# A shorter inverse root in the norm, and weights, rows and empty steps placed otherwise, in a two-layer encoder

## The chip, the core and the metric

The kernel runs on one core of a Trainium2 chip. The metric is the device time of one execution in microseconds. A core has five engines that work side by side, each through its own queue of instructions in a fixed order: PE (TensorE, matrix products; its weight loads are shown as PEld), DVE (VectorE), ACT (ScalarE), POOL (GpSimd), and SP (SyncE), which here issues most of the transfers between memory and the core. An instruction starts when those ahead of it in its queue have been taken and what it waits for is there.

## The reference

Two groups of tokens, a prompt of 512 and a sample of 1024, pass through two layers with the same weights. All data are fp32 and 1024 features wide. One layer is:

```python
hn = rmsnorm(h, ln1[i])
z = hn @ w_in[i]
q, k, v, ga, uf, gf, mga, mgf = jnp.split(z, SPLIT_IDX, axis=-1)
a = band_attention(rope(q), rope(k), v, sink[i]) * jax.nn.silu(ga)   # 8 heads of 64, band of 128
f = fourier_mix(uf, w_fmix[i]) * jax.nn.silu(gf)                     # Re(FFT2) in 4 groups of 128
merged = sigmoid(mga) * (a @ w_ao[i]) + sigmoid(mgf) * (f @ w_fo[i])
h = h + merged @ w_out[i]
h = h + (p[i] @ w_pe[i]) * sigmoid(rmsnorm(h, ln_pg[i]) @ w_pg[i])
```

with `rmsnorm(x, g) = x * rsqrt(mean(x*x) + 1e-6) * g`, and a last rmsnorm behind the second layer.

## The kernel before

The tokens are three chunks of 512: chunk 0 is the prompt, chunks 1 and 2 are the sample and are called the pair. A tile is 128 features by 512 tokens, so a chunk has 8 tiles, and a weight of 128 outputs has 8 pieces of 128x128.

**Products in three parts.** An fp32 operand is split into a high part, cast by ACT (L89), and a low part, the difference from it, by DVE and for some weights by POOL (L90). A product is then three matmuls into one bank of PSUM: high by high (L101), high by low (L102), low by high (L103). So each weight and each activation needs one ACT and one DVE (or POOL) instruction of 128x512 before PE can use it. `Weights` does that for a stream of weights: `get` hands out weight i, loads weight i + 3 and splits weight i + 2 (L175 to L180).

**The stages.** In each layer come, in this order: the prompt's input projection with 34 weight tiles (`project_prompt`, some 45 to 285 us in layer 0 and 1142 to 1374 in layer 1); the pair's input projection (286 to 682, 1375 to 1771); and the merges of the branches, the output projection and the gate, first for the prompt, then for the pair, the pair's being the end of the program. The pair's projection multiplies its two chunks by two weight tiles at once in seven products instead of eight (L232), with the sums of weights S1 to S4 (L209 to L216) and the sums of activations T1 to T4 (`pair_parts`). `Pair.prepare(n)` makes and splits the weight operands up to the n-th of the order A11, S2, S1, S3, A12, A22, S4. `pair_made` makes the activations by rows: row k joins features k and k + 4 of the two chunks; it normalises four pieces (`pinned`, L390, or `normed`, L361) and makes seven operands. A product needs all four rows.

**Side work.** `run` lets a main generator go step by step and moves others along with it, each from a given step on and at a given rate. Beside the prompt's projection go, in turn, the pair's norm, rows 0 and 1, and then a chain of the prompt's attention, its Fourier part and row 2; row 3 comes behind the projection.

**The order on each engine.** The framework's scheduler puts the instructions of each engine in order by its own model of time; the order of the code is its priority. `keep_in_program_order` holds an instruction where the code has it (as in `pinned`), and `issue_after` lets it come only after a given one. Buffers are rings (45 tiles "act", 16 "scr", 12 "tiny", 20 "stat"), so an instruction can also wait for a buffer's last reader.

**The norm.** `Norm.add` sums the squares of the 8 tiles of a chunk. In `stats_steps` PE sums over features into a few columns (L333, L335), DVE computes the inverse root there, PE spreads it by transposes (L350), and DVE copies it (L356) for the normalisations. The inverse root is 12 operations on 128x4 or 128x2: adding eps (L339), a first guess from the bits (L341, L342), and three Newton steps of three operations (L344 to L346). There are 16 such chains in the program. The last chunk's tail is worked in two halves of 256 tokens, with its gate at L633 to L638 and its results at L662.

**Other names in the rows.** L371, L372, L378, L383: the sums of `pair_parts`. L420 to L423 (`roped`): the rotary embedding, of which L422 multiplies by the sines. L467, L468, L473: the gates of the prompt's projection. L828, L836, L863, L868: the attention's scores, their maximum, the transposes of the probabilities and the product with the values. L985 to L991: the Fourier part's products, L1046 its last sums on DVE and L1051 its gate on POOL. L239, L243, L249: sums of the pair's products. L598 to L602: gate and addition in the merges.

## Time and profile before

| what | value |
|---|---|
| runs | 2205.24, 2209.6, 2211.03 us; median 2209.6 |
| profiled execution | 2210.05 us, of which the span that the profile shows is 2208.3 |
| PE, matmuls | 2167.4 us busy, 98% of the span |
| DVE | 1501.5 us, 68% |
| ACT | 1090.1 us, 49% |
| POOL | 297.3 us, 13% |
| mean granted clock of PE | 0.995 of full speed |
| moved by transfers | 380.71 MB, mean 172 GB/s |

The profile is of one execution. A row of a timeline gives the start of a group of like instructions in us from the span's start, how long the group lasts, the engine, the line of the kernel, the operation, its output and inputs by pool (act, scr, tiny, misc, mm, sc, o), the shape, and the number of instructions; in brackets stands the engine's idle time just before and what ended it. Matmuls overlap in the pipeline, so a row lasts longer than the distance to the next. PE is the busiest engine by far, and the others matter where PE waits for them.

### The profile page before, as it was taken

What the parts mean: (1) busy time and instruction counts of PE and PEld (TensorE: products, weight loads), DVE (VectorE), ACT (ScalarE), POOL (GpSimd) and SP (SyncE); (2) the same over time, 40 slices, a digit from 0 to 9 for tenths busy, and PEclk for the clock granted to TensorE, in tenths of its full rate; (3) what the DMA queues carried; (4) which work ended last, traced back from release to release, by engine and by line L of the source; (5) the groups of instructions that cost most, each with busy time, mean ns of one, the idle gap of its engine ahead of it and who ended that gap; (6) DMA issues with size and microseconds to landing.
All of it is one profiled execution on the core that took longest, in us unless ns stands there. A gap on an engine that the chain in (4) does not pass through costs nothing. (4 is left out here: it accounts for less than half of the span.)

```text
span 2208.3 us, 30143 instructions
## 1 busy us (share of the span) xinstructions
PE 2167.4 (98%) x10242; PEld 1803.6 (82%) x10242; DVE 1501.5 (68%) x2896; ACT 1090.1 (49%) x2333; POOL 297.3 (13%) x216
## 2 busy tenths in 40 slices
PE   9999999999999999999999999999999999999997
PEld 7778877888888887888888888788888888888886
DVE  5866676776778883464557665867766787864386
ACT  5476433666665454124324854336666644612352
POOL 0201100000002111312400010100000011241141
PEclk9999999999999999999999999999999999999998
DMA  8565554444448575632356555443444574753143
GB/s 316 202 191 196 172 169 163 167 131 150 148 143 289 202 257 183 218 105 65 137 162 208 156 186 180 162 163 129 155 145 153 200 273 146 250 201 119 60 146 100
DMA packets 242170, 380.71 MB, mean 172 GB/s; under 512 B 21216, under 2 KB 97632, under 8 KB 242016
## 3 DMA queue, kind: packets, MB, share of 16 engines
q1 hardware_dynamic: 235104, 366.19, 49.1%
q10 hardware_dynamic: 6912, 12.59, 1.5%
q8 instruction: 81, 1.33, 0.2%
q14 instruction: 73, 0.60, 0.1%
HBM read 270.17 MB, written 108.53 MB: 171 GB/s over the span
## 5 line engine op out<-in xcount | busy, mean ns | idle before, releaser
L232 PE MATMUL mm<-act,act 128*128 128x512 f32 x2856 | 693.5, 393 | 7.1 <-ACT act L89 3.7
L232 PEld LDWEIGHTS mm<-act,act 128*128 128x128 f32 x2856 | 530.4, 188 | 117.2 <-ACT act L89 6.9
L101 PE MATMUL mm<-act,act 128*128 128x512 f32 (+1 forms) x1392 | 546.3, 393 | 6.2 <-ACT act L89 1.8
L103 PE MATMUL mm<-act,act 128*128 128x512 f32 (+1 forms) x1392 | 545.3, 392 | 3.7 <-DVE act L90 3.7
L102 PE MATMUL mm<-act,act 128*128 128x512 f32 (+1 forms) x1392 | 544.1, 391 | 0.0
L89 ACT CAST act<-act 128x512 fp32r<-128x512 f32 x574 | 329.5, 619 | 196.4 <-DMA act<-in_w_af 60.1
L90 DVE TENSOR_TENSOR act<-act,act 128x512 fp32r<-128x512 f32 x474 | 330.6, 732 | 24.3 <-ACT act L89 22.8
L103 PEld LDWEIGHTS mm<-act,act 128*128 128x128 f32 x1392 | 262.6, 189 | 60.1 <-DVE act L90 7.5
L101 PEld LDWEIGHTS mm<-act,act 128*128 128x128 f32 x1392 | 262.8, 189 | 59.6 <-ACT act L89 2.8
L102 PEld LDWEIGHTS mm<-act,act 128*128 128x128 f32 x1392 | 262.6, 189 | 51.5
L89 ACT CAST act<-scr 128x512 fp32r<-128x512 f32 (+1 forms) x260 | 152.9, 615 | 132.9 <-DVE scr L423 69.6
L90 DVE TENSOR_TENSOR act<-scr,act 128x512 fp32r<-128x512 f32 x256 | 179.1, 720 | 55.0 <-ACT act L89 53.7
L90 POOL TENSOR_TENSOR act<-act,act 128x512 fp32r<-128x512 f32 x100 | 142.8, 1453 | 324.4 <-ACT act L89 292.8
L321 ACT ACTIVATE scr<-act 128x512 f32<-128x512 f32 x103 | 63.8, 632 | 216.7 <-DVE act L582 142.9
L877 POOL TENSOR_TENSOR scr<-scr,scr 128x512 f32<-128x512 f32 x24 | 34.0, 1415 | 873.1 <-DVE scr L874 828.6
L90 DVE TENSOR_TENSOR act<-misc,act 128x512 fp32r<-128x512 f32 x132 | 88.2, 686 | 71.9 <-ACT act L89 71.7
L89 ACT CAST act<-misc 128x512 fp32r<-128x512 f32 x132 | 73.8, 587 | 122.2 <-PE misc L863 120.5
L839 ACT ACTIVATE act<-act,stat 128x385 f32<-128x385 f32 (+1 forms) x192 | 110.5, 579 | 35.8 <-DVE stat L836 35.2
L836 DVE CUSTOM_DVE_ANT_0 act<-sc,mask_sb,nsink_sb 128x384 f32<-128x384 f32 (+1 forms) x192 | 104.4, 569 | 32.1 <-PE sc L828 31.6
L101 PE MATMUL sc<-act,act 128*128 128x512 f32 (+1 forms) x316 | 118.6, 375 | 1.2 <-ACT scr L785 1.2
L102 PE MATMUL sc<-act,act 128*128 128x512 f32 (+1 forms) x316 | 118.1, 374 | 0.0
L103 PE MATMUL sc<-act,act 128*128 128x512 f32 (+1 forms) x316 | 117.9, 373 | 0.0
(222 smaller groups left out, 2622.2 us busy)
## 6 DMA issues: line engine op xcount, KB each, us to landing
act<-in_w_in SPq DMA_DIRECT2D x136, 256.0 KB, 4.7
act<-in_w_in SPq DMA_DIRECT2D x68, 512.0 KB, 4.4
gt<-scr SPq DMA_DIRECT2D x96, 256.0 KB, 2.7
scr<-gt SPq DMA_DIRECT2D x96, 256.0 KB, 5.4
act<-in_w_pg SPq DMA_DIRECT2D x80, 256.0 KB, 3.8
act<-in_w_af SPq DMA_DIRECT2D x64, 256.0 KB, 5.4
act<-in_w_out SPq DMA_DIRECT2D x64, 256.0 KB, 4.9
pl<-scr ACTq DMA_DIRECT2D x48, 256.0 KB, 3.0
```

The lines of the kernel that those rows point to most:

```text
L89: S.copy(hi, src)
L90: lo_eng.tensor_tensor(lo, src, f(hi), op=ALU.subtract)
L101: keep(PE.matmul(out, wh, xh, start=i == 0, stop=False))
L102: PE.matmul(out, wh, xl, start=False, stop=False)
L103: PE.matmul(out, wl, xh, start=False, stop=i == n - 1)
L232: PE.matmul(bank, w, v, start=first and k == 0 and n == 0, stop=k == 3 and n == 2, skip_group_check=True)
L321: S.activation(sq, h, AF.Square)
L836: V.tensor_tensor_reduce(out=pr[:, :W], in0=sc[:, :W], in1=msk, scale=-0.125, scalar=nsink_sb[:, l, head : head + 1], op0=ALU.add, op1=ALU ...
L839: S.activation(pr, pr, AF.Exp, bias=nmx[:, e], scale=-1.0, accum_out=rs[:, e])
L877: G.tensor_tensor(a2, a2, gate, op=ALU.mult)
```

## The change

- `Weights.get` splits weight i + 2 before it issues the load of weight i + 3; before, it was the other way round.
- `Norm`: eps is added once, in one of the wide accumulations on DVE (there is a flag for it), and the inverse root takes 8 small operations instead of 12: a first guess in one operation, one step of higher order with fitted constants in four, and one Newton step in three. It uses one more small tile.
- `pair_normed`: the normalisations of row 2 keep the place that the code gives them, as those of rows 0 and 1 do. Before, they were only held behind the row before.
- `roped`: the product with the sines (L422) of the pair's chunks goes to DVE; the prompt's stays on POOL. That is 8 instructions.
- In the prompt's attention four empty steps stand behind the first unit's scores.
- `first_weights` prepares the pair's first weight operands up to S3 in its last step, where before it stopped at S2.
- In `run`, rows 0 and 1 start at step 30 instead of 24, and the chain that begins with attention at step 42 instead of 44.

```diff
--- before.py
+++ after.py
@@ -175,8 +175,8 @@
         def get(self):
             i = self.at
             self.at += 1
+            self.split(i + 2)
             self.load(i + 3)
-            self.split(i + 2)
             return self.w.pop(i)
 
     class Pair:
@@ -310,7 +310,7 @@
 
     class Norm:
         def __init__(self):
-            self.acc = None
+            self.acc, self.has_eps = None, False
 
         def add(self, h, eng=V):
             if self.acc is None:
@@ -319,7 +319,11 @@
             else:
                 sq = scr()
                 S.activation(sq, h, AF.Square)
-                eng.tensor_tensor(self.acc, self.acc, sq, op=ALU.add)
+                if eng is V and not self.has_eps:
+                    V.scalar_tensor_tensor(self.acc, self.acc, D * EPS / P, sq, op0=ALU.add, op1=ALU.add)
+                    self.has_eps = True
+                else:
+                    eng.tensor_tensor(self.acc, self.acc, sq, op=ALU.add)
 
         def stats(self):
             for _ in self.stats_steps(range(4)):
@@ -334,16 +338,20 @@
                 if rest is not None:
                     PE.matmul(st[:, i : i + 1], rest[:, i * P : (i + 1) * P], mean_sb, start=False, stop=True)
 
-            v, y, z = (st[:, 4 * j : 4 * j + n] for j in range(1, 4))
-            self.r = r = sbt([P, n], F32, "tiny")
-            yield keep(V.tensor_scalar(v, st[:, 0:n], EPS, None, op0=ALU.add))
-
-            yield keep(V.tensor_scalar(y.bitcast(I32), v.bitcast(I32), 1, None, op0=ALU.arith_shift_right))
-            yield keep(V.tensor_scalar(r.bitcast(I32), y.bitcast(I32), -1.0, float(0x5F3759DF), op0=ALU.mult, op1=ALU.add))
-            for _ in range(3):
-                yield keep(V.tensor_tensor(z, v, r, op=ALU.mult))
-                yield keep(V.scalar_tensor_tensor(z, z, -0.5, r, op0=ALU.mult, op1=ALU.mult))
-                yield keep(V.scalar_tensor_tensor(r, z, 1.5, r, op0=ALU.add, op1=ALU.mult))
+            v, z, w = st[:, 0:n], st[:, 4 : 4 + n], st[:, 8 : 8 + n]
+            assert self.has_eps
+            self.r, q = sbt([P, n], F32, "tiny"), sbt([P, n], F32, "tiny")
+            r = self.r
+
+
+            yield keep(V.tensor_scalar(r.bitcast(I32), v.bitcast(I32), -0.5, float(0x5F113500), op0=ALU.mult, op1=ALU.add))
+            yield keep(V.tensor_tensor(z, v, r, op=ALU.mult))
+            yield keep(V.tensor_tensor(q, z, r, op=ALU.mult))
+            yield keep(V.scalar_tensor_tensor(w, q, -2.25339258, q, op0=ALU.add, op1=ALU.mult))
+            yield keep(V.scalar_tensor_tensor(r, w, 2.28257789, r, op0=ALU.add, op1=ALU.mult))
+            yield keep(V.tensor_tensor(z, v, r, op=ALU.mult))
+            yield keep(V.scalar_tensor_tensor(z, z, -0.5, r, op0=ALU.mult, op1=ALU.mult))
+            yield keep(V.scalar_tensor_tensor(r, z, 1.5, r, op0=ALU.add, op1=ALU.mult))
 
         def scale_ps(self, rb_ps, n=4):
             for j in range(n):
@@ -395,7 +403,7 @@
             hs = [[tile(i, kk) for i in range(2)] for kk in (k, k + 4)]
             for j in range(2):
                 for i in range(2):
-                    if k < 2:
+                    if k < 3:
                         pinned(hs[j][i], k + 4 * j, gain, rbs[i])
                     else:
                         with tc.issue_after(x["last"]):
@@ -419,7 +427,7 @@
             a, b = scr(), scr()
             V.tensor_tensor(a, out, self.rope[c, i][:, 0, :], op=ALU.mult)
             V.stream_shuffle(b, out, [j ^ 8 if i else j ^ 1 for j in range(32)])
-            G.tensor_tensor(b, b, self.rope[c, i][:, 1, :], op=ALU.mult)
+            (V if c else G).tensor_tensor(b, b, self.rope[c, i][:, 1, :], op=ALU.mult)
             V.tensor_tensor(a, a, b, op=ALU.add)
             return halves(a, V)
 
@@ -894,6 +902,9 @@
             yield from scores(u)
             if u:
                 yield from values(u - 1)
+            else:
+                for _ in range(4):
+                    yield
         yield
         yield from values(len(units) - 1)
 
@@ -1150,12 +1161,12 @@
             yield
             pairs.prepare(0)
             yield
-            pairs.prepare(1)
+            pairs.prepare(3)
 
         run(project_prompt(l, parts, ws, first_weights()), [
             (make, 8 if l == 0 else 10, 0.7 if l == 0 else 0.35),
-            (pair_made(xs, l, range(2)), 24, 1.0),
-            (chain(attention(l, (0,), False), fourier(l, 0), pair_made(xs, l, range(2, 3))), 4 * MT_U + 4, 2.1),
+            (pair_made(xs, l, range(2)), 30, 1.0),
+            (chain(attention(l, (0,), False), fourier(l, 0), pair_made(xs, l, range(2, 3))), 4 * MT_U + 2, 2.1),
         ])
         for _ in pair_made(xs, l, range(3, 4)):
             pass
```

Lines of the changed kernel from the norm on are higher by 8: L356 is L364, L390 is L398, L361 is L369, L371, L372, L378, L383 are L379, L380, L386, L391, and L468 is L476; L1046 is L1057.

The first place is DVE in the prompt's projection of layer 0, around 96 us. act_890 and act_885 are the raw tenth weight tile of w_in (before and now), and the two L90 that read it are its low parts; scr_870 and scr_877, now scr_861 and scr_868, are the pair's spread inverse roots. Before:

```order
L390 SCALAR_TENSOR_TENSOR act_623<-act_623,ln_sb,scr_877 128x512
L390 SCALAR_TENSOR_TENSOR act_631<-act_631,ln_sb,scr_877 128x512
L90 TENSOR_TENSOR act_918<-act_621,act_918 128x512
L371 TENSOR_TENSOR scr_916<-act_623,act_621 128x512
L372 TENSOR_TENSOR scr_917<-act_631,scr_916 128x512
L378 TENSOR_TENSOR act_623<-act_631,act_623 128x512
L468 SCALAR_TENSOR_TENSOR scr_935<-scr_935,mm_899 128x512
L468 SCALAR_TENSOR_TENSOR scr_988<-scr_988,mm_950 128x512
L468 SCALAR_TENSOR_TENSOR scr_1037<-scr_1037,mm_1004 128x512
L90 TENSOR_TENSOR act_938<-scr_917,act_938 128x512
L90 TENSOR_TENSOR act_944<-act_890,act_944 128x512
L90 TENSOR_TENSOR act_947<-act_890,act_947 128x512
```

Now:

```order
L90 TENSOR_TENSOR act_879<-act_802,act_879 128x512
L90 TENSOR_TENSOR act_882<-act_802,act_882 128x512
L90 TENSOR_TENSOR act_918<-act_885,act_918 128x512
L90 TENSOR_TENSOR act_921<-act_885,act_921 128x512
L364 COPY scr_861<-misc_856 128x512
L364 COPY scr_868<-misc_863 128x512
L398 SCALAR_TENSOR_TENSOR act_618<-act_618,ln_sb,scr_861 128x512
L476 SCALAR_TENSOR_TENSOR scr_915<-scr_915,mm_888 128x512
L398 SCALAR_TENSOR_TENSOR act_620<-act_620,ln_sb,scr_868 128x512
L398 SCALAR_TENSOR_TENSOR act_626<-act_626,ln_sb,scr_861 128x512
L398 SCALAR_TENSOR_TENSOR act_628<-act_628,ln_sb,scr_868 128x512
L476 SCALAR_TENSOR_TENSOR scr_959<-scr_959,mm_927 128x512
```

The two subtractions of the tenth tile stood behind the first row's pieces and three gates; now they stand behind those of the ninth tile (act_802) and ahead of the copies.

The second place is DVE at the end of the prompt's projection of layer 0, from 281 us on. scr_2904 and scr_2984 are S1 and S3 before, scr_2895 and scr_2905 are S1 and S3 now; scr_2944, scr_2943, act_627, act_633, act_635 belong to the pair's last row (now scr_2943, scr_2942, act_624 and so on). Before:

```order
L378 TENSOR_TENSOR act_627<-act_635,act_627 128x512
L213 TENSOR_TENSOR scr_2984<-act_2835,act_2836 128x512
L90 TENSOR_TENSOR act_2950<-scr_2944,act_2950 128x512
L90 TENSOR_TENSOR act_2953<-scr_2943,act_2953 128x512
L90 TENSOR_TENSOR act_2957<-act_627,act_2957 128x512
L90 TENSOR_TENSOR act_2960<-act_633,act_2960 128x512
L383 TENSOR_TENSOR act_633<-act_633,scr_2944 128x512
L243 TENSOR_TENSOR scr_3018<-mm_2979,scr_3001 128x512
L90 TENSOR_TENSOR act_2964<-act_633,act_2964 128x512
L90 TENSOR_TENSOR act_2967<-act_635,act_2967 128x512
L90 TENSOR_TENSOR act_2981<-scr_2904,act_2981 128x512
L90 TENSOR_TENSOR act_2986<-scr_2984,act_2986 128x512
```

Now:

```order
L210 TENSOR_TENSOR scr_2896<-scr_2895,act_2826 128x512
L213 TENSOR_TENSOR scr_2905<-act_2826,act_2827 128x512
L90 TENSOR_TENSOR act_2899<-scr_2896,act_2899 128x512
L90 TENSOR_TENSOR act_2902<-scr_2895,act_2902 128x512
L216 TENSOR_TENSOR scr_2896<-act_2826,scr_2896 128x512
L90 TENSOR_TENSOR act_2907<-scr_2905,act_2907 128x512
L90 TENSOR_TENSOR act_2944<-act_622,act_2944 128x512
L379 TENSOR_TENSOR scr_2942<-act_624,act_622 128x512
L380 TENSOR_TENSOR scr_2943<-act_632,scr_2942 128x512
L386 TENSOR_TENSOR act_624<-act_632,act_624 128x512
L90 TENSOR_TENSOR act_2949<-scr_2943,act_2949 128x512
L90 TENSOR_TENSOR act_2952<-scr_2942,act_2952 128x512
```

The low parts of S1 and S3 stood behind the whole last row; now they stand ahead of it, right behind that of S2 (scr_2896).

The third place is DVE at the end of the prompt's Fourier part, around 247 us: act_625, act_627, act_633, act_635 are the four pieces of row 2 before, and act_622, act_624, act_630, act_632 now. Before, their first normalisations stood in the work of row 1, at 115 us:

```order
L90 TENSOR_TENSOR act_1111<-act_629,act_1111 128x512
L383 TENSOR_TENSOR act_629<-act_629,scr_1041 128x512
L361 SCALAR_TENSOR_TENSOR act_625<-act_625,ln_sb,scr_870 128x512
L361 SCALAR_TENSOR_TENSOR act_627<-act_627,ln_sb,scr_877 128x512
L361 SCALAR_TENSOR_TENSOR act_633<-act_633,ln_sb,scr_870 128x512
L361 SCALAR_TENSOR_TENSOR act_635<-act_635,ln_sb,scr_877 128x512
L90 TENSOR_TENSOR act_1121<-act_629,act_1121 128x512
L90 TENSOR_TENSOR act_1130<-act_631,act_1130 128x512
```

Now they stand behind the last sums of the Fourier part:

```order
L1054 TENSOR_TENSOR scr_2580<-scr_2569,scr_2570 128x128
L1055 TENSOR_TENSOR scr_2580<-scr_2569,scr_2570 128x127
L1057 TENSOR_TENSOR scr_2580<-scr_2569,scr_2570 128x127
L398 SCALAR_TENSOR_TENSOR act_622<-act_622,ln_sb,scr_861 128x512
L398 SCALAR_TENSOR_TENSOR act_624<-act_624,ln_sb,scr_868 128x512
L398 SCALAR_TENSOR_TENSOR act_630<-act_630,ln_sb,scr_861 128x512
L398 SCALAR_TENSOR_TENSOR act_632<-act_632,ln_sb,scr_868 128x512
L379 TENSOR_TENSOR scr_2604<-act_624,act_622 128x512
L90 TENSOR_TENSOR act_2606<-act_622,act_2606 128x512
L380 TENSOR_TENSOR scr_2605<-act_632,scr_2604 128x512
```

They have left the stretch of rows 0 and 1, and are new between the Fourier part and the operands of row 2.

## Rows read from the trace of the kernel before

**Rows 1.** The page, busy time of each engine: us (share of the span), and its instructions.

```profile
PE 2167.4 (98%) x10242; PEld 1803.6 (82%) x10242; DVE 1501.5 (68%) x2896; ACT 1090.1 (49%) x2333; POOL 297.3 (13%) x216
```

**Rows 2.** The list of PE's waits, grouped by the line that waits and the one that ended the wait: us in total, times, the longest.

```profile
PE o L868 <- ACT act L89: 4.0, 4, 1.5
PE mm L103 <- DVE act L90: 3.7, 5, 1.0
PE mm L232 <- ACT act L89: 3.7, 4, 1.1
...
PE mm L232 <- DVE act L90: 1.6, 2, 1.0
```

**Rows 3.** Windows of 8 us in the prompt's projection of layer 0: busy time of PE, PEld, DVE, ACT and POOL, each with its number of instructions, then the granted clock of PE, the share of the DMA engines and GB/s.

```profile
96.00:104.00 8.00, 6.81 (x16) 5.08 (x17) 7.28 (x13) 4.49 (x9) 0.00 (x0) 0.57 0.90 293
...
112.00:120.00 8.00, 8.00 (x37) 6.64 (x36) 7.96 (x14) 4.73 (x13) 0.00 (x0) 1.00 1.00 310
120.00:128.00 8.00, 8.00 (x39) 6.69 (x38) 1.34 (x5) 1.10 (x4) 0.00 (x0) 1.00 0.95 325
```

**Rows 4.** The timeline of PE around 96 us, and at 123 us.

```profile
94.13 0.39 PE L103 MATMUL mm<-act,act 128*128 128x512 f32 x1
96.29 0.50 PE L101 MATMUL mm<-act,act 128*128 128x512 f32 x1 [1.77 <-ACT act L89]
...
97.92 0.79 PE L103 MATMUL mm<-act,act 128*128 128x512 f32 x1 [0.90 <-DVE act L90]
...
98.94 0.63 PE L102 MATMUL mm<-act,act 128*128 128x512 f32 x1
...
104.71 0.39 PE L102 MATMUL mm<-act,act 128*128 128x512 f32 x1
...
105.85 0.39 PE L101 MATMUL mm<-act,act 128*128 128x512 f32 x1
...
123.10 0.40 PE L103 MATMUL mm<-act,act 128*128 128x512 f32 x1
```

**Rows 5.** The timeline of DVE in the same stretch: the copies of the inverse roots, the tenth tile's low parts, and row 2's first normalisations.

```profile
88.40 1.29 DVE L356 COPY scr<-misc 128x512 f32<-128x512 f32 x2 [4.46 <-PE misc L350]
...
97.18 1.28 DVE L90 TENSOR_TENSOR act<-act,act 128x512 fp32r<-128x512 f32 x2
...
115.30 2.74 DVE L361 SCALAR_TENSOR_TENSOR act<-act,ln_sb,scr 128x512 f32<-128x512 f32 x4
```

**Rows 6.** The timeline of PE at the start of the pair's projection in layer 0.

```profile
291.90 1.26 PE L232 MATMUL mm<-act,act 128*128 128x512 f32 x4 [0.77 <-ACT act L89]
294.16 0.96 PE L232 MATMUL mm<-act,act 128*128 128x512 f32 x3 [1.00 <-DVE act L90]
```

**Rows 7.** The timelines of DVE and ACT there: the low part of S2, those of S1 and S3, and on ACT the last gate of the prompt's projection.

```profile
281.43 0.69 DVE L90 TENSOR_TENSOR act<-scr,act 128x512 fp32r<-128x512 f32 x1 [13.39 <-ACT act L89]
...
293.42 1.29 DVE L90 TENSOR_TENSOR act<-scr,act 128x512 fp32r<-128x512 f32 x2
...
285.79 0.60 ACT L473 ACTIVATE scr<-mm 128x512 f32<-128x512 f32 x1 [3.88 <-PE mm L103]
```

**Rows 8.** The timelines of PE, DVE and POOL in the pair's projection of layer 0, where the rope of a chunk is made.

```profile
336.40 1.95 PE L232 MATMUL mm<-act,act 128*128 128x512 f32 x7 [1.06 <-ACT act L89]
...
332.20 1.78 DVE L213 TENSOR_TENSOR scr<-act,act 128x512 f32<-128x512 f32 x1
...
334.50 0.68 DVE L423 TENSOR_TENSOR scr<-scr,scr 128x512 f32<-128x512 f32 x1
...
331.94 1.48 POOL L422 TENSOR_TENSOR scr<-scr,act 128x512 f32<-128x512 f32 x1 [7.09 <-DVE scr L421]
```

**Rows 9.** The timelines of PE in and behind the prompt's Fourier part in both layers, of DVE and POOL at its end in layer 0, and a window there with the columns of rows 3.

```profile
231.14 0.33 PE L103 MATMUL sc<-act,scr 128*128 128x128 f32 x1 [0.35 <-DVE scr L90]
...
1312.25 0.70 PE L985 MATMUL misc<-act,scr 128*128 128x256 f32 x2 [0.60 <-ACT scr L89]
...
259.09 0.50 PE L103 MATMUL mm<-act,act 128*128 128x512 f32 x1 [0.98 <-DVE act L90]
...
249.23 1.62 DVE L90 TENSOR_TENSOR act<-scr,act 128x512 fp32r<-128x512 f32 x1
...
248.17 2.13 POOL L1051 TENSOR_TENSOR scr<-scr,scr 128x512 f32<-128x512 f32 x1 [7.30 <-DVE scr L1046]
...
246.00:262.00 16.00, 15.02 (x66) 11.89 (x65) 15.87 (x32) 10.50 (x20) 2.13 (x1) 1.00 0.64 215
```

**Rows 10.** The timelines of PE and DVE at the chains of the inverse root in the last merge: the sums that a chain begins from and the transposes that wait for it, and on DVE the first operation of the last chain but one, the gate between its operations, and the first and the last operation of the last chain.

```profile
2127.17 0.95 PE L333 MATMUL misc<-mean_sb,scr 128*128 128x1 f32 x8
...
2141.35 0.62 PE L350 MATMUL misc<-ident_sb,tiny 128*128 128x128 f32 x4 [1.50 <-DVE tiny L346]
...
2192.44 0.16 DVE L339 TENSOR_SCALAR misc<-misc 128x2 f32<-128x2 f32 x1
...
2193.91 0.41 DVE L633 TENSOR_TENSOR scr<-mm,scr 128x256 f32<-128x256 f32 x1
...
2197.75 0.17 DVE L339 TENSOR_SCALAR misc<-misc 128x2 f32<-128x2 f32 x1 [0.41 <-PE misc L335]
...
2199.95 0.16 DVE L346 SCALAR_TENSOR_TENSOR tiny<-misc,tiny 128x2 f32<-128x2 f32 x1
```

## The prediction, made before the changed kernel was timed

> **What bounds the kernel now.** I read the page first, then the list of PE's waits, then windows around the places that the list names, then timelines of PE, DVE, ACT and POOL there. PE (TensorE) is busy 2167.4 us of a span of 2208.3 [rows 1]: all its idle time is 40.9 us, and no edit of work on other engines can give more than that and what the clock loses after an idle stretch. The list of waits [rows 2] shows what this idle time is made of: stalls of at most 1.5 us, almost all for an operand that ACT has just cast (L89) or DVE has just subtracted (L90). The greatest knot lies at 96 us: two stalls, and then matmuls whose rows last 0.63 instead of 0.39; the granted clock of that window is 0.57, so much of it runs at 1.2 GHz, between stretches at 2.4 [rows 3, 4]. The profiled execution took 2210.05 and its span 2208.3, so 1.75 lie around the span, which the change doesn't touch; it lies 0.45 above the median of the runs, 2209.6. The sum is made against 2210.05.
>
> In a clean stretch matmuls of 512 columns start 0.228 apart ((105.85 - 104.71) / 5 [rows 4]) though each row lasts 0.39, so a stall shown as idle time x costs x + 0.16.
>
> **Weights split ahead of loads, rows later (term A).** The product that begins at 96.29 is that of the tenth w_in tile of layer 0, 24 matmuls. The last one before it starts at 94.13; without a stall the next product, now at 105.85, would begin 25 x 0.228 = 5.7 after that, at 99.8. The knot costs 6.0. What PE waits for is a cast and a subtraction that stand on ACT and DVE behind the pair's first row (L371, L372, L378) and L468; the DVE piece is done only at 98.4 [rows 5]. In the new order both stand right behind the tile before, ahead of the copies of 88.40. They are ready before 94.4, and the knot goes: -6.0. What is late next? DVE is full until 120 [rows 3], so whatever goes ahead pushes something back. From those copies to the last split of this stretch, the fourteenth tile's, stand 44 instructions in the new order. At 0.61 each (two L90 take 1.28 where one takes 0.68 [rows 5]) that is 26.8, so it is ready at 115.2. PE's first use of it, at 123.10 now [rows 4], would come at 117.1. There are 1.9 us to spare, because row 2's first four normalisations, 2.74 at 115.30 [rows 5], have left this stretch. The attention's loads issue earlier too, no longer behind a store that waits for DVE. I take the whole 6.0; the other bound is 0, all of it waited for later.
>
> **The pair's weights ahead (term B).** At 291.90 and 294.16 PE waits for the S1 and S3 weights, cast and subtracted after the last row [rows 6, 7]; with the same place in layer 1, two of the four waits of L232 for L89, 0.77 each, and the two for L90, 1.6 in all [rows 2]. That is 3.1 of idle time, and 4 x 0.16: 3.8. Now they stand directly behind S2's, whose subtraction starts at 281.43 after 13.39 us of idle DVE [rows 7]. This moves the last row's pieces back by 3 x 0.6 = 1.8, but their casts stand anyway behind an ACT instruction that waits for PE until 285.79 [rows 7], and PE takes products whose data are ready in between. I take 3.8; bounds 1.5 and 3.8.
>
> **The rope's product on DVE (term C).** At 336.40, and in layer 1, PE waits 1.06 for casts that stand on ACT behind the cast of the rope's sum, L423 [rows 8]. POOL's L422 lasts 1.48 there, and L213 on DVE beside it 1.78 instead of 0.68. On DVE the product costs 0.6, and L213 gets back 1.1. But DVE takes the product itself, and in the new order L423 stands behind L243, another 0.6: no gain from here. The same exchange one unit earlier has the same 1.1 to give back and only the 0.6 to pay, and L423 no longer waits for POOL. Followed through with DVE's waits for PE and ACT, L423 ends some 0.7 earlier: 2 x 0.7 = 1.4, bounds 0 and 2 x 1.22.
>
> **Rows and the Fourier part (terms D and E).** Row 2's normalisations now stand behind the Fourier part's last operations, with one subtraction that was far ahead of them: 2.7 + 0.6 = 3.3 us on DVE, right ahead of the splits for which PE already waits 0.98 at 259.09 [rows 9], and so in layer 1. Against it, PE's last Fourier groups come 12 matmuls earlier in the order, 2.7 us, and with them POOL's L1051. The difference, 0.6 in each layer, is waited for there: +1.2. Bounds: -2.2 (both stalls gone) and, if the 2.7 do not come through, +6.6. At 231.14 and 1312.25 PE waits 0.35 and 0.60 [rows 9] for pieces of Fourier groups whose first matmuls now come up to 13 places earlier: 1.3 with twice 0.16, of which I take half, -0.6; bounds 0 and 1.3.
>
> The Trainium skill, "SBUF — State Buffer", section "Who interferes with whom", says that a VectorE instruction with two SBUF inputs and a GpSimd one that reads SBUF exclude each other for a whole instruction, whichever started first. Here L90 at 249.23 lasts 1.62 instead of 0.68 beside POOL's L1051, which lasts 2.13 [rows 9]. By the rule row 2's normalisations, with two SBUF inputs each, could be held for up to those 2.13, so term D would be up to 1.2 per layer dearer and the sum 2199.4; by the row one instruction pays 0.9, and it pays that before as well. I go by the row.
>
> **Norm (term F).** 12 small operations become 8. They are 0.20 apart where nothing lies between ((2199.95 - 2197.75) / 11 [rows 10]), so a chain is 0.8 shorter; of 16 chains PE stands waiting for three. At 2141.35 it waits 1.50 for a chain whose sums were ready at 2128 [rows 10]: the operations stand between splits, and the splits were late, slowed beside POOL like the one at 249.23. In the new order the chain before it ends and its tiles are finished ahead of those splits, and this chain spans 18 rows, ten wide ones of 0.61 and eight of 0.1 to 0.2; begun at 2128.3 it is over at some 2135.5, five microseconds before PE asks. The stall goes: -1.7; the other bound is -0.4, half a chain between wide rows. At the end two chains stand on the path itself. The first is 0.8 shorter, but L633, now at 2193.91 between its operations, stands behind all eight, at 2192.44 + 8 x 0.20 = 2194.04, 0.13 later; the last is 0.8 shorter: -0.7. The other 13 run beside matmuls at full rate and cost PE nothing, a cover that holds while the chain's end is ahead of PE's L350; where it didn't, these three are. Adding eps in the accumulate is one wide operation for another. The four empty steps and the start numbers leave the order at the first attention unit as it was, so attention's waits (4.0 for L868 [rows 2]) stay: 0.
>
> Sum: -6.0 - 3.8 - 1.4 + 1.2 - 0.6 - 1.7 - 0.7 = -13.0, so 2197.
>
> **Rivals.**
> 1. The knot at 96 only moves. For: DVE is full until 120, and the first attention unit behind it is a chain of DVE and ACT. Against: from 120 to 128 DVE is busy 1.34 of 8 us [rows 3], so nothing queues there. It would give 6.0 back: 2203.
> 2. DVE is the bound of the whole prompt projection, and what is put ahead is always waited for later. Place: the splits behind row 2, at 246 to 262 and in layer 1. For: DVE works 15.87 of 16 us there [rows 9]. Row 2's 3.3 and two instructions held by POOL (1.9) would come in full, 0.98 + 5.2 = 6.2 of idle PE. Two stalls of 2.7 together were followed by 1.2 GHz at 98 [rows 4], of which 6.0 - 3.0 = 3.0 were the clock's; so 8.2 per layer, 16.4 in all, with A not gained: 2210.05 - (13.0 + 1.2 - 6.0) + 16.4 = 2218, slower. Against: the order shows the Fourier groups 12 matmuls earlier. It decides if the last L1046, which is followed by L1051 at 248.17 now, is not ended before 246.5.
> 3. The change doesn't do what it says for weights and rows: the pieces stand earlier in the order, but start when their buffers come free. Then only C and F are left: 2206.2. Against: PE, which frees them, is long past the tiles in question.
> 4. More goes than I count: as everything behind 105 comes 6 us earlier and the attention's loads earlier still, half of the 4.0 for L868 closes, and D's two stalls too: 2197 - 2.0 - 3.4 = 2191.6.
>
> **How the numbers follow.** My forecast 0.62; its own range, from the bounds of B, C, E and F and the skill's price for D, is 2192 to 2202. Rival 1: 0.16, rival 2: 0.06, rival 3: 0.08, rival 4: 0.08. A measurement of this kernel can tell about 0.3% from no change, 6.6 us: faster means under 2203.0, slower over 2216.2. Faster: 0.62 + 0.08 + half of rival 1 = 0.78. Slower: rival 2, 0.06. Same: 0.16. The range reaches to rivals 1, 3 and 4: 2190 to 2206; outside lie rival 2 and the edges of the rest, under 2 in 10.
>
> **What would show it.** In the profile of the changed kernel: A is right if the granted clock from 85 to 105 is 1.00 and no stall over 0.3 us stands between 90 and 120, wrong if a wait of some microseconds for L90 stands at 110 to 136. B: no wait for L89 or L90 in the first 10 us of either pair projection. C: waits of some 0.4 left there 40 us later. D: waits for L90 near 250 and 1340 of 1.6 each; over 3, with a dip of the clock, speaks for rival 2. F: no wait of the second merge's L350, and 8 rows 0.20 apart before the last L350. The prediction is wrong as a whole if PE's idle time falls by less than 6 us.

## The result, and the profile after

The changed kernel takes 2194.54 us (median of four runs, 2193.75 to 2195.63), the one before in the same comparison 2209.32; the ratio is 0.9936, 95% interval 0.9919 to 0.9953. The forecast was 2197 in 2190 to 2206, faster: it holds. The profiled execution took 2194.6, its span 2192.7, so 15.45 less than the 2210.05 that the sum was made against (forecast 13.0).

The page and the list of PE's waits of the changed kernel, columns as in [rows 1, 2]; L868 is now L876, L473 is L481. Behind them stands the line of L473 from the list of before:

```profile
PE 2163.5 (99%) x10242; PEld 1804.0 (82%) x10242; DVE 1485.1 (68%) x2840; ACT 1089.1 (50%) x2333; POOL 282.2 (13%) x208
```

```profile
PE o L876 <- ACT act L89: 4.1, 4, 1.5
PE mm L101 <- ACT scr L481: 2.8, 4, 1.1
PE mm L103 <- DVE act L90: 1.9, 4, 0.6
...
PE mm L232 <- ACT act L89: 0.7, 2, 0.4
```

```profile
PE mm L101 <- ACT scr L473: 1.7, 3, 0.7
```

PE's idle time falls from 40.9 to 2192.7 - 2163.5 = 29.2, by 11.7; the other 3.9 are busy time that went: fewer matmuls ran at 1.2 GHz. L232's waits for casts fall from 3.7 to 0.7, its waits for L90 are off the list, and L103's are halved. The attention's 4.0 stay. The second line has grown: PE waits for L481, ScalarE's tanh that empties a PSUM bank of the projection, four times instead of three, and the one of 1.07 at 202 is new.

Windows, columns as in [rows 3]:

```profile
96.00:104.00 8.00, 8.00 (x37) 6.64 (x36) 7.08 (x13) 4.85 (x10) 0.00 (x0) 1.00 0.82 249
112.00:120.00 8.00, 8.00 (x39) 6.69 (x38) 4.22 (x10) 4.14 (x13) 0.00 (x0) 1.00 0.43 135
...
200.00:215.00 15.00, 13.93 (x71) 11.91 (x70) 10.90 (x35) 9.99 (x27) 3.92 (x6) 0.89 0.82 281
...
246.00:262.00 16.00, 14.86 (x64) 11.36 (x63) 13.94 (x23) 10.41 (x20) 0.00 (x0) 1.00 0.75 251
```

The knot is gone: clock 1.00 where it was 0.57, and DVE, full until 120 before, is half idle from 112 on. In its place a smaller dip stands at 200 to 215, with 0.89. The timeline of PE shows both, and the places of terms B, C and D:

```profile
94.16 0.39 PE L103 MATMUL mm<-act,act 128*128 128x512 f32 x1
94.39 0.39 PE L101 MATMUL mm<-act,act 128*128 128x512 f32 x1
...
202.04 0.79 PE L101 MATMUL mm<-act,act 128*128 128x512 f32 x1 [1.07 <-ACT scr L481]
202.63 0.63 PE L102 MATMUL mm<-act,act 128*128 128x512 f32 x1
...
254.78 0.50 PE L101 MATMUL mm<-act,act 128*128 128x512 f32 x1 [0.74 <-ACT act L89]
...
255.90 0.50 PE L103 MATMUL mm<-act,act 128*128 128x512 f32 x1 [0.39 <-DVE act L90]
...
286.62 3.56 PE L232 MATMUL mm<-act,act 128*128 128x512 f32 x15
...
330.21 1.03 PE L232 MATMUL mm<-act,act 128*128 128x512 f32 x3 [0.36 <-ACT act L89]
```

Product follows product at 94.16 without a break (1.77 before [rows 4]); the pair's projection begins without one (0.77 and 1.00 [rows 6]); the rope's place keeps 0.36 of 1.06 [rows 8].

On DVE, the ninth and tenth tiles' low parts (four L90) now end before the copies, as the order said. The chain of the second merge begins at 2116.47, which is 2129.3 on the clock of before (12.87 of lead there), and is over 3.9 us before PE's transposes, which start at 2127.49 without a wait. The last chain is eight rows 0.20 apart:

```profile
82.11 2.50 DVE L90 TENSOR_TENSOR act<-act,act 128x512 fp32r<-128x512 f32 x4
86.84 1.29 DVE L364 COPY scr<-misc 128x512 f32<-128x512 f32 x2 [2.23 <-PE misc L358]
...
2116.47 0.15 DVE L347 TENSOR_SCALAR tiny<-misc 128x4 int32<-128x4 int32 x1
...
2123.48 0.15 DVE L354 SCALAR_TENSOR_TENSOR tiny<-misc,tiny 128x4 f32<-128x4 f32 x1
...
2183.03 0.16 DVE L347 TENSOR_SCALAR tiny<-misc 128x2 int32<-128x2 int32 x1 [0.32 <-PE misc L339]
...
2184.42 0.16 DVE L354 SCALAR_TENSOR_TENSOR tiny<-misc,tiny 128x2 f32<-128x2 f32 x1
```

**Where the 15.5 us came from.** The n-th matmul of a line and shape is the same work in every kernel here, so its start in before less its start in another kernel is that kernel's lead. The table gives by how much the lead grows in each stretch (median over the matmuls within 7 us of its two ends, times of before), from one profile of each kernel; the stretches left out add up to 1.2 at most. A row belongs to the profiled execution, which need not be the median one. The medians come from several comparisons, in which the kernel before had medians from 2207.26 to 2209.32, so two of them are good to some 2 us. e1 to e12 are the experiments below. In the bottom row stands the forecast by its terms.

| kernel | median us | 60-112 knot | 112-185 attention | 185-272 Fourier, row 2 | 272-400 pair, rope | 790-900 gate | 1190-1262 attention | 1262-1365 Fourier, row 2 | 1365-1500 pair, rope | 2100-2172 merge | tail |
|---|---|---|---|---|---|---|---|---|---|---|---|
| changed | 2194.5 | 6.1 | 0.0 | -2.8 | 3.0 | 3.6 | -0.9 | 1.5 | 2.6 | 1.7 | 1.0 |
| e1 | 2200.2 | 4.7 | -0.1 | -2.2 | 2.9 | 3.6 | -0.8 | -1.4 | 2.6 | 1.7 | 1.4 |
| e2 | 2194.3 | 6.0 | 1.5 | -3.0 | 3.0 | 0.6 | -0.7 | -1.3 | 2.6 | 1.7 | 1.1 |
| e3 | 2198.8 | 6.1 | -0.2 | -0.9 | 2.9 | 2.2 | -0.9 | 1.4 | 2.6 | 1.7 | -1.7 |
| e4 | 2206.6 | 6.0 | -3.5 | -7.4 | 3.0 | 3.3 | -1.0 | -1.7 | 2.6 | 1.7 | 1.7 |
| e5 | 2208.0 | 0.1 | 0.0 | -1.3 | 3.0 | 2.2 | -0.8 | -2.2 | 2.6 | 1.7 | -1.6 |
| e6 | 2201.7 | 6.1 | -0.1 | -1.7 | 0.4 | 3.6 | -0.9 | -0.3 | 0.1 | 1.7 | 1.7 |
| e7 | 2212.4 | 6.1 | -4.9 | -9.0 | 2.9 | 3.5 | -4.5 | -1.7 | 2.6 | 1.7 | 1.7 |
| e8 | 2194.3 | 6.0 | 1.5 | -2.7 | 3.0 | 3.6 | -0.9 | -1.7 | 2.6 | 1.7 | 1.4 |
| e9 | 2196.3 | 6.1 | 0.0 | -1.8 | 2.9 | 3.6 | -0.7 | -2.0 | 2.6 | 1.7 | 1.7 |
| e10 | 2193.0 | 6.1 | 0.0 | 0.4 | 3.0 | 3.6 | -0.9 | -0.8 | 2.6 | 1.7 | 1.7 |
| e11 | 2192.0 | 6.1 | -0.6 | 0.1 | 3.0 | 3.6 | -0.9 | 3.6 | 2.6 | 1.7 | 1.0 |
| e12 | 2191.9 | 6.1 | -0.6 | 2.5 | 3.0 | 3.6 | -0.9 | -0.5 | 2.6 | 1.7 | 1.7 |
| forecast | 2197 | 6.0 | 0 | -0.3 | 2.6 | 0 | 0 | -0.3 | 2.6 | 1.7 | 0.7 |

The columns of the knot, the pair and rope, and the merge repeat to 0.1 us in every kernel that keeps their edits. The two of the Fourier part and row 2 don't: they hold stretches at 1.2 GHz that come in one profile and not in the next (below), and in layer 1 a wait of PE for a cast, 2.67 us near 1333 in e1, e5 (at 1340) and e9 and 1.78 in e8, that the changed kernel does not have. So a difference of 2 or 3 us there between two single profiles decides little.

### The profile page after: what moved, and what is told of

Same layout as the page of the kernel before. It is cut to its first block, busy times and chain, and to the rows that moved or that the text cites. A ratio compares the mean times of both kernels' runs of the same rounds, so it can differ in the third digit from the quotient of the medians.

```text
span 2192.7 us, 30077 instructions
## 1 busy us (share of the span) xinstructions
PE 2163.5 (99%) x10242; PEld 1804.0 (82%) x10242; DVE 1485.1 (68%) x2840; ACT 1089.1 (50%) x2333; POOL 282.2 (13%) x208
## 5 line engine op out<-in xcount | busy, mean ns | idle before, releaser
L232 PE MATMUL mm<-act,act 128*128 128x512 f32 x2856 | 692.6, 392 | 2.5 <-DVE scr L249 1.7
L232 PEld LDWEIGHTS mm<-act,act 128*128 128x128 f32 x2856 | 530.9, 188 | 111.1 <-ACT act L89 2.7
L103 PE MATMUL mm<-act,act 128*128 128x512 f32 (+1 forms) x1392 | 543.5, 391 | 1.9 <-DVE act L90 1.9
L89 ACT CAST act<-act 128x512 fp32r<-128x512 f32 x574 | 328.8, 618 | 181.0 <-DMA act<-in_w_af 70.9
L90 DVE TENSOR_TENSOR act<-act,act 128x512 fp32r<-128x512 f32 x474 | 322.6, 715 | 34.3 <-ACT act L89 32.5
L103 PEld LDWEIGHTS mm<-act,act 128*128 128x128 f32 x1392 | 262.0, 188 | 56.8 <-DVE act L90 4.4
L89 ACT CAST act<-scr 128x512 fp32r<-128x512 f32 (+1 forms) x260 | 152.7, 615 | 128.1 <-DVE scr L431 58.0
L90 DVE TENSOR_TENSOR act<-scr,act 128x512 fp32r<-128x512 f32 x256 | 174.4, 702 | 51.0 <-ACT act L89 49.5
L90 POOL TENSOR_TENSOR act<-act,act 128x512 fp32r<-128x512 f32 x100 | 140.9, 1437 | 311.5 <-ACT act L89 279.4
L90 DVE TENSOR_TENSOR act<-misc,act 128x512 fp32r<-128x512 f32 x132 | 88.1, 685 | 72.0 <-ACT act L89 71.6
L89 ACT CAST act<-misc 128x512 fp32r<-128x512 f32 x132 | 73.9, 587 | 121.4 <-PE misc L871 119.1
L844 DVE CUSTOM_DVE_ANT_0 act<-sc,mask_sb,nsink_sb 128x384 f32<-128x384 f32 (+1 forms) x192 | 104.2, 568 | 29.8 <-PE sc L836 29.2
L103 PE MATMUL sc<-act,act 128*128 128x512 f32 (+1 forms) x316 | 118.0, 373 | 0.0
```

The lines of the kernel that those rows point to most:

```text
L89: S.copy(hi, src)
L90: lo_eng.tensor_tensor(lo, src, f(hi), op=ALU.subtract)
L103: PE.matmul(out, wl, xh, start=False, stop=i == n - 1)
L232: PE.matmul(bank, w, v, start=first and k == 0 and n == 0, stop=k == 3 and n == 2, skip_group_check=True)
L844: V.tensor_tensor_reduce(out=pr[:, :W], in0=sc[:, :W], in1=msk, scale=-0.125, scalar=nsink_sb[:, l, head : head + 1], op0=ALU.add, op1=ALU ...
```

## Experiments: the knot at 96

**e1, rows 0 and 1 start at 24 again.**

```diff
-            (pair_made(xs, l, range(2)), 30, 1.0),
+            (pair_made(xs, l, range(2)), 24, 1.0),
```

> The changed kernel (2194.6) with one number back: rows 0 and 1 of the pair's operands start at 24 instead of 30. Everything else stays, the split ahead of the load too. Theory: the knot at 96 us was opened by the later start alone; with 24 the tenth tile's split stands on VectorE again behind the first four normalisations, the row's sums and two wide operations of other tiles, so a stall of some us with a stretch at 1.2 GHz comes back between 90 and 105: 4 to 6 us lost there and nothing elsewhere, 2198.5 to 2200.5. Rival: splitting ahead of the load opened it; then the knot stays gone and the time is within 1 us of 2194.6.

Measured: 2200.21 us, ratio 0.996 (0.9945 to 0.9975). The time is what the theory said, and the theory is wrong: of the 6.1 only 1.4 came back at the knot, and no row at 1.2 GHz. The timelines of PE and of DVE there:

```profile
95.98 0.50 PE L103 MATMUL mm<-act,act 128*128 128x512 f32 x1 [0.76 <-DVE act L90]
96.32 0.39 PE L101 MATMUL mm<-act,act 128*128 128x512 f32 x1
```

```profile
87.06 1.29 DVE L364 COPY scr<-misc 128x512 f32<-128x512 f32 x2 [3.41 <-PE misc L358]
...
95.25 1.28 DVE L90 TENSOR_TENSOR act<-act,act 128x512 fp32r<-128x512 f32 x2
```

The tenth tile's low parts stand behind the row again, as before, yet at 95.25 instead of 97.18 [rows 5]: the copies come 1.3 earlier (the two chains in front have 8 operations less), and one gate less stands between. Another 2.9 were lost in layer 1 behind the Fourier part, where PE waits 2.67 for a cast at 1333.87. That is no part of the knot: e9, which has the rows at 30, waits as long there. The profiled execution is the fastest of the four, 2198.12; what the median has beyond it was not traced.

**e2, the load ahead of the split again.**

```diff
-            self.split(i + 2)
             self.load(i + 3)
+            self.split(i + 2)
```

> The changed kernel with the next tile's load ahead of the next split again, nothing else undone. Theory: the knot at 96 stays gone (the start of the rows did it), but the 3.6 us that were gained between 818 and 851 without having been forecast come back as lost, because on SyncE's queue the loads of the gate's tiles (the DMAs of the line that fetches pl) fall back behind the weights' loads and the stores that wait: 2197.5 to 2199, with VectorE waiting about 2 us for such a DMA near 837. Rival 1: the order of split and load is what opened the knot: 2199 to 2201 with a stall at 90 to 100. Rival 2: both gains come from elsewhere: within 1 us of 2194.6.

Measured: 2194.25 us, 0.9938 (0.9923 to 0.9953). That is the same time as the changed kernel's and below the theory's range; by the time alone rival 2 would hold. The profile, of the slowest of the four runs (2198.91), has both effects that the theory names. The knot stays gone: with the later start and the shorter chain in place, the order of split and load has no part in it. And 3.0 of the 3.6 at 790 to 900 are lost, of which attention gives 1.5 back. DVE waits for the fetch of pl, the gate's operand (L608's input), in e2 as in before (there L600), and PE behind it for the banks. First before, then e2, in each DVE ahead of PE (in before with the gate ahead of the one that waits, and the splits in front of it):

```profile
837.47 1.29 DVE L90 TENSOR_TENSOR act<-act,act 128x512 fp32r<-128x512 f32 x2 [0.61 <-ACT act L89]
838.68 1.78 DVE L600 SCALAR_TENSOR_TENSOR scr<-scr,scr 128x512 f32<-128x512 f32 x1
...
845.47 0.69 DVE L600 SCALAR_TENSOR_TENSOR scr<-scr,scr 128x512 f32<-128x512 f32 x1 [1.93 <-DMA scr<-pl]
...
850.80 0.50 PE L101 MATMUL mm<-act,act 128*128 128x512 f32 x1 [1.58 <-ACT scr L785]
```

```profile
837.77 0.69 DVE L608 SCALAR_TENSOR_TENSOR scr<-scr,scr 128x512 f32<-128x512 f32 x1 [2.06 <-DMA scr<-pl]
...
843.10 0.51 PE L101 MATMUL mm<-act,act 128*128 128x512 f32 x1 [1.59 <-ACT scr L793]
```

The fetch is held up on SP's queue (a helper's store is L280, pl's fetch L597 and now L605). Before, then e2, then the changed kernel, the last with its gate and the split in front of it on DVE:

```profile
842.18 0.33 SPq L280 DMA_DIRECT2D h<-act  x1
842.60 0.88 SPq L597 DMA_DIRECT2D scr<-pl  x2
```

```profile
834.35 0.33 SPq L280 DMA_DIRECT2D h<-act  x1
834.79 0.85 SPq L605 DMA_DIRECT2D scr<-pl  x2
```

```profile
830.59 0.33 SPq L280 DMA_DIRECT2D h<-act  x1
831.01 0.38 SPq L605 DMA_DIRECT2D scr<-pl  x1
...
827.16 1.60 DVE L90 TENSOR_TENSOR act<-act,act 128x512 fp32r<-128x512 f32 x1
828.68 0.68 DVE L608 SCALAR_TENSOR_TENSOR scr<-scr,scr 128x512 f32<-128x512 f32 x1
```

Counted from the start of the merge, it is the same fetch (the seventh) behind the same store (the sixth) in all three, and that store goes out in each when the result of the sixth gate is there. What the order of split and load moved is the gate: before and in e2 four splits stand on DVE between the fifth and the sixth gate, in the changed kernel one, with the other three behind the gate's first operation. So the gate ends, the store goes and the fetch behind it goes 842.60 - 831.01 - 6.9 = 4.7 us sooner (6.9 is the lead there), and DVE's wait for it is gone. In e2, whose lead there is 7.8, the fetch is back to the tenth at its time of before (834.79 + 7.8 = 842.6).

**e3, twelve operations again.**

```diff
-                if eng is V and not self.has_eps:
...
+                eng.tensor_tensor(self.acc, self.acc, sq, op=ALU.add)
...
-            yield keep(V.tensor_scalar(r.bitcast(I32), v.bitcast(I32), -0.5, float(0x5F113500), op0=ALU.mult, op1=ALU.add))
...
+            for _ in range(3):
+                yield keep(V.tensor_tensor(z, v, r, op=ALU.mult))
```

> The changed kernel with the twelve small operations of the inverse root back, and eps no longer in the accumulation; all else as changed. Theory: 1.0 us lost at the end (two chains), 0 to 1.7 at the second merge's norm near 2128 (the order of the chain against the splits stays as changed, so rather 0), and nothing at 818 to 851: 2195.6 to 2197.3. Rival: the shorter chain gave what was gained at 818 to 851 and at 2141 as well, 3.6 + 1.7 + 1.0: 2200.9.

Measured: 2198.79 us, 0.9957 (0.9942 to 0.9972), above the theory's range and below the rival; the profiled execution is the fastest of the four, 2197.24. The tail loses 2.7 (two chains of 0.8, and 1.10 of a new wait ahead of them), the gate stretch 1.4, in a wait of 1.08 at 811.51. The second merge loses nothing: an early place in the order is enough there, even for twelve operations (the chain begins at 2115.84). It is not needed either: in e2 the chain begins only at 2124.30, which with the lead of 8.3 there is 2132.6 on the clock of before, 1 us from its old place (2133.60), but its eight operations are over in 2.5 us, and the 1.7 stay gained. Which edit gave it the early place was not found, and no run has the load first and the long chain together. Nor does the knot come back.

**e5, both e1's and e3's edits undone.**

```diff
-            (pair_made(xs, l, range(2)), 30, 1.0),
+            (pair_made(xs, l, range(2)), 24, 1.0),
...
+            for _ in range(3):
+                yield keep(V.tensor_tensor(z, v, r, op=ALU.mult))
```

> The changed kernel with both undone that e1 and e3 undid apart: rows 0 and 1 start at 24, and the inverse root has its twelve operations. The split stays ahead of the load. Theory: either edit alone opens the knot at 96 us, because each puts the tenth tile's split some us earlier (the two interleaved chains by 24 - 16 = 8 operations of 0.2, 1.6 us; the later start by putting the split ahead of the copies). With both undone VectorE's order there is that of before, and the knot is back whole: about 6 us lost by 105, on top of the 4.3 of e3's time: some 2204. Rival: the split ahead of the load had a part in it as well; then less than 3 us are lost there, 2198 to 2201.

Measured: 2208.02 us, 1.0007 (0.9997 to 1.0016). The knot is back whole, 0.1 of 6.1 left, with the idle times of [rows 4] to the hundredth:

```profile
96.92 0.50 PE L101 MATMUL mm<-act,act 128*128 128x512 f32 x1 [1.77 <-ACT act L89]
...
98.55 0.79 PE L103 MATMUL mm<-act,act 128*128 128x512 f32 x1 [0.90 <-DVE act L90]
99.14 0.63 PE L101 MATMUL mm<-act,act 128*128 128x512 f32 x1
```

So the later start alone opens the whole knot (e3), the shorter chain alone 4.7 of 6.1 (e1), and undoing them one at a time would have credited them with 1.4 and nothing. The split ahead of the load, which e5 keeps, opens none of it alone. The time is 4.0 us beyond the expected 2204; compared with e3, 3.6 are lost at 1262 to 1365, with PE's wait of 2.67 at 1340 as in e1.

## Experiments: the other terms

**e6, terms B and C undone.**

```diff
-            (V if c else G).tensor_tensor(b, b, self.rope[c, i][:, 1, :], op=ALU.mult)
+            G.tensor_tensor(b, b, self.rope[c, i][:, 1, :], op=ALU.mult)
...
-            pairs.prepare(3)
+            pairs.prepare(1)
```

> The changed kernel with the pair's weights behind the rows again (prepare(1)) and the rope's product on GpSimd again. Theory: the two terms are separate and come back each at its own place: about 2.1 us lost at the beginning of either pair projection (stalls of 0.8 and 0.6 to 1.0 for ScalarE's cast and VectorE's subtraction), and 0.7 lost some 40 us behind it (a stall of 1.06 where 0.36 stands now): 2 x (2.0 + 0.7) = 5.4, so 2200. Rival: VectorE has less in its way there now, so the pair's weights come in time even behind the rows: 2196.

Measured: 2201.69 us, 0.9973 (0.9964 to 0.9983). In the two columns 0.5 is left of 5.6. PE's timeline of layer 0 has the three stalls at their old places:

```profile
287.66 1.26 PE L232 MATMUL mm<-act,act 128*128 128x512 f32 x4 [0.77 <-ACT act L89]
289.55 10.29 PE L232 MATMUL mm<-act,act 128*128 128x512 f32 x44 [0.63 <-DVE act L90]
...
331.81 3.54 PE L232 MATMUL mm<-act,act 128*128 128x512 f32 x14 [1.06 <-ACT act L89]
```

**e4, e7 and e9, the start and the empty steps.** e4 puts the start back, e7 takes the empty steps out, e9 does both.

```diff
-                for _ in range(4):
-                    yield
...
-            (chain(attention(l, (0,), False), fourier(l, 0), pair_made(xs, l, range(2, 3))), 4 * MT_U + 2, 2.1),
+            (chain(attention(l, (0,), False), fourier(l, 0), pair_made(xs, l, range(2, 3))), 4 * MT_U + 4, 2.1),
```

> The changed kernel with the start of the first attention unit, the Fourier part and row 2 put back by two places (4 * MT_U + 4), the four empty steps kept. Theory: the stall of 1.07 us at 202 us for ScalarE's tanh of a tile (L481), which stands behind the Fourier part's casts, and the 1.2 GHz stretch behind it go, since in this order that tanh stands ahead of the casts: 2.5 us gained there, 2192. Rival: the stall belongs to ScalarE being full there and comes back at the next tile or in layer 1: 2194 to 2196.

> The changed kernel without the four empty steps behind the first unit's scores (the start stays at 4 * MT_U + 2). Theory: the number of steps between the start and the Fourier part decides how its casts on ScalarE meet the tanh of the main stream's tiles; without the empty steps the scores of the second unit and everything behind them come four steps, about 2 tiles of the projection, earlier, the first unit's values come sooner after their scores, so the stall of 1.5 us at 128 for their casts (and that of 0.9 before it) grows by 1 to 3 us in each layer: 2197 to 2200. Rival: attention gains from an earlier second unit what the Fourier part loses: within 1.5 us of 2194.6.

> The changed kernel with both halves of that pair undone: no empty steps and the start at 4 * MT_U + 4, as before the change. e4 (start alone put back) was 11 us slower, e7 (empty steps alone taken out) 18. Theory: two places of the projection and four empty steps at 2.1 steps a place stand for the same shift, so what follows the first unit's scores meets the projection's tiles as in the changed kernel; the pair is worth nothing in time: 2193.5 to 2196. Rival: it is the earlier scores of the first unit that the change gains by, and without them the stalls at 125 to 130 and at 1210 grow: 2197 to 2200.

Measured: e4 2206.55 us, 0.9991 (0.9982 to 1.0001); e7 2212.44, 1.0021 (1.0012 to 1.0031); e9 2196.3, 0.995 (0.9933 to 0.9967). For e4 theory and rival both fell: the wait for L481 went as expected, but attention and the Fourier part of layer 0 lost 8 us net of that, spread over many places, part of it to the clock (0.79 granted at 168 to 176, 0.72 at 205 to 217), and layer 1 another 3. e7 lost more than expected, and not by longer stalls at 128 alone. The windows of e7 in layer 0, columns as in [rows 3], show it: over 60 us of attention PE is 55.49 busy, where the changed kernel has 59.43, and the clock behind is 0.77.

```profile
140.00:200.00 60.00, 55.49 (x277) 45.24 (x276) 32.79 (x81) 41.74 (x106) 2.82 (x3) 1.00 0.50 157
200.00:215.00 15.00, 13.65 (x55) 10.61 (x55) 10.62 (x25) 7.42 (x22) 5.02 (x7) 0.77 0.68 233
```

e9 is 0.3 above its theory's range and below the rival: the two edits cancel (four empty steps at 2.1 a place are 1.9 places, the start moves by 2), and the pair is worth nothing that the runs can tell. That each half alone puts the steps of attention out of step with the tiles of the projection fits this, but no run here separates it from other causes.

**e8, the load first for layer 0's prompt weights alone.**

```diff
+    ws.load_first = True
...
+            if self.load_first:
+                self.load(i + 3)
+                self.split(i + 2)
```

> The changed kernel with the next load ahead of the split only for layer 0's prompt weights, and the split ahead for all later streams. e2 showed layer 0's first 260 us 1.2 us shorter with the load first, but lost 3.0 at 840 and 2.6 at 1305, both in later streams. Theory: places are independent, so the 1.2 stay gained and the 5.6 are not lost: span 2191.5, time 2193.4. Rival: layer 0's order carries over into later pools and queues: a loss elsewhere, 2194 to 2197.

Measured: 2194.3 us, 0.9943 (0.9928 to 0.9958). The range of the rival. Attention keeps e2's 1.5, the gate stretch its 3.6, and layer 1's Fourier stretch gives 3 back, with PE's wait of 1.78 there. No better than the changed kernel.

**e10, an empty step ahead of the Fourier part.**

```diff
-            (chain(attention(l, (0,), False), fourier(l, 0), pair_made(xs, l, range(2, 3))), 4 * MT_U + 2, 2.1),
+            (chain(attention(l, (0,), False), iter([None]), fourier(l, 0), pair_made(xs, l, range(2, 3))), 4 * MT_U + 2, 2.1),
```

> The changed kernel with one empty step more, between the first attention unit's last piece and the Fourier part. In this order ScalarE's tanh of the projection tile (L481) stands ahead of the four casts that it stood behind at 201.37. Theory: PE's wait for it at 202.04 (1.07) goes and with it the eight matmuls at 1.2 GHz behind it: 2.5 us gained from 200 to 210, nothing lost elsewhere but at most 0.5 at the row 2 splits: 2192 to 2192.5. Rival: the tiles meet the casts one place later, so a stall of about 1 us for L481 or a cast comes at 215 to 230 or in layer 1, or the row 2 splits come later than PE asks for them: 2194 to 2198.

Measured: 2192.99 us, 0.9931 (0.9917 to 0.9946). The time lies between theory and rival. The wait for L481 at 202 is gone, and the stretch is 3.2 better in layer 0; 2.3 of that are lost in layer 1. As theory and rival say, each in its layer.

**e11, row 2's normalisations free.**

```diff
-                    if k < 3:
+                    if k < 2:
```

> The changed kernel with row 2's four normalisations in each layer no longer kept in their place (k < 2, as before): VectorE runs them again behind row 1's last difference, ahead of the first attention unit. Theory: they take 2.74 us of a VectorE that is full until 113 and has 4 us free behind it, so the last split ahead of attention comes up to 2.7 later and PE waits up to 0.8 there in layer 0; against it the splits of the rows behind the Fourier part come 2.7 earlier, and the stalls of 0.74 and 0.39 near 255 and of 0.58 at 1338 go: 1.5 gained, 2193 to 2195. Rival: VectorE's place behind row 1 is full, and a knot of several us with a stretch at 1.2 GHz comes between 115 and 125: 2197 to 2200.

Measured: 2192.0 us, 0.9926 (0.9911 to 0.9941). Below the theory's range. Ahead of attention it costs 0.6. Behind the Fourier part PE no longer waits, in either layer (the window of e11, then its timeline at L481):

```profile
246.00:262.00 16.00, 16.00 (x72) 13.25 (x71) 12.92 (x22) 9.06 (x16) 0.00 (x0) 1.00 0.73 250
```

```profile
202.20 0.50 PE L101 MATMUL mm<-act,act 128*128 128x512 f32 x1 [1.08 <-ACT scr L481]
202.54 0.39 PE L102 MATMUL mm<-act,act 128*128 128x512 f32 x1
```

So that line of the change costs something at its places: the stalls of 0.74, 0.39 and, in layer 1, 0.58, with 3 x 0.16 for the restarts 2.2, less the 0.6, is 1.6; the medians differ by 2.5.

**e12, e10's and e11's edits together.**

```diff
-                    if k < 3:
+                    if k < 2:
...
-            (chain(attention(l, (0,), False), fourier(l, 0), pair_made(xs, l, range(2, 3))), 4 * MT_U + 2, 2.1),
+            (chain(attention(l, (0,), False), iter([None]), fourier(l, 0), pair_made(xs, l, range(2, 3))), 4 * MT_U + 2, 2.1),
```

> The changed kernel with what e10 and e11 did apart: row 2's normalisations not kept in their place, and one empty step ahead of the Fourier part. Theory: the two have different places. e11 gained 4.8 at the splits of the rows behind the Fourier part (2.0 in layer 0, the rest in layer 1 by 1340) and keeps PE's wait for L481 at 202 and the 1.2 GHz stretch behind it; e10 took just that away, 2.5. Together 2187.9 - 2.5 = 2185.4 of span, time 2187.2; ratio to before 0.9905. Rival: part of what either gained is the same slack of ScalarE and VectorE between 200 and 260 and is not to be had twice, or layer 1 gives back some 2 us as in e10: 2189 to 2192.

Measured: 2191.88 us over five runs, 0.9925 (0.9911 to 0.9938). The rival: layer 0 adds up (2.5 where e11 has 0.1), and layer 1 gives 4 back, with two waits of 1.2 and 1.3 for the Fourier part's small cast and subtraction (L940, L941) at 1303 to 1305. e10 to e12 have medians 1.5 to 2.7 below the changed kernel's, under 0.3%, and their intervals overlap its own: they are not told apart from it.

## Why the prediction was right

**The knot (A, -6.0): right, 6.1.** The split stood where the order said, and what it pushed back was not missed: DVE is half idle from 112 on, attention's column is 0.0, and rival 1 falls with that. What the step had wrong is the edit: "weights split ahead of loads" opens none of it alone (e5) and is not needed (e2); the later start opens all of it, and the eight operations less alone 4.7 (e1, e3, e5).

**Pair's weights and rope (B -3.8, C -1.4): right,** 5.6 in the two columns against 5.2; e6 takes them away at their places. The waits of 0.36 that stay after C are the 0.4 named in advance.

**Rows and Fourier part (D +1.2, E -0.6): the sum was off.** It said 0.6 lost in all; the two columns say -2.8 + 1.5, 1.3 lost. Row 2's waits were smaller than the 1.6 foretold (0.74 + 0.39 and 0.58) and of the right cause (e11). But the step left two things out for the Fourier groups that come earlier. Their casts also moved ahead of L481 on ACT, and PE waited 1.07 for the bank it empties; with the slow matmuls behind it that was 2.5 of layer 0's 2.8. And E's half of two waits was not gained: the waits of 0.35 and 0.60 are gone, but 0.78 and 0.59 stand in that part now. The 0.78 is for L941, a subtraction of 128x2 that takes 0.91 instead of 0.15 beside POOL's L1062 (last section). The 1.5 of layer 1 are luck: before's own dip at 1295, worth 1.6, didn't come.

**Norm (F): right in size.** -1.7 at the second merge is 1.7. The early place that the step counted on is enough, as e3 and e5 keep it with twelve operations, but it is not needed with eight (e2). The tail's -0.7 is 1.0. The step "the other 13 cost PE nothing" fails for one: of the 3.6 at 790 to 900, 1.4 go with the long chain (e3).

**What the sum had not: the gate, 3.6.** The prediction read the list of waits as "at most 1.5 us, almost all" for L89 or L90. The whole list adds up to 33.0 us, of which those two have 16.9, and it has waits of 2.5 (L346), 1.8 (L89) and 1.6 (L785); that 1.6 and the 0.7 for L598 are the gate's. The step on the weights followed their split to the knot, not to the merges, where three splits that now stand behind the gate let its store and a fetch behind that go 4.7 us sooner (e2, 3.0). That the total came within 2.5 us is in part luck: this gain and the dip at 1295 that didn't come hid the loss at L481, which is itself 1.6 of clock that eight other kernels with the same wait don't pay, and 0.9 in layer 1's attention. That 0.9 is in nearly all kernels run here; 0.5 of it is a longer wait of the scores (L836) for L844, 0.87 instead of 0.35, and why that one is longer was not found.

**The range.** The bounds that it names don't add up to 2192 to 2202: B, C, E and F at their bounds and the price for D give 2195.3 to 2205.0, and 2192 is reached only with D's own bound of -2.2.

**Attention's 0 for start and steps: right in net, blind in each half.** e9 confirms the nothing, but each half alone costs 12 and 18 us (e4, e7); a reader who had met either edit alone and priced it at 0 would have been far off.

**Rivals 2 to 4.** DVE works 13.94 of 16 us at 246 to 262, and PE waits 1.13 there, not 6. The pieces start where the order has them. L876's waits stay at 4.1, so nothing of rival 4's attention gain came.

## What to carry to other kernels

When one of two edits may remove a stall, undo both as well as each: a redundant pair hides from every single test, and a pair that cancels looks like nothing. When a load moves in the code, follow its split on the engines and the queue that issues it, up to the first instruction there that waits, and ask what that one waits for. A short operation with both inputs in SBUF is dear beside POOL: place it where POOL is idle. The chain's operations here that read PSUM did not stretch. Compare leads at the same work, stretch by stretch: e1 had the forecast time for the wrong reason, and only that view showed it.
